# Values of heads 0 and 1 by seven half-size products, with the scores between them

## The chip, the cores and the metric

The kernel runs on one core of one Trainium2 chip. The metric is the device time of one execution in microseconds (us). Engines are named as the profile names them: PE is TensorE (matmul), PEld its weight load, DVE is VectorE, ACT is ScalarE, POOL is GpSimd, SP is the engine that issues the loads. L975 is line 975 of the kernel before.

## The reference, cut to what matters

One layer of a hybrid block over 528 tokens (16 meta tokens and 512 of the sequence), model width 1024:

```python
xn = rms_norm(h, norm_mix_g[l])
z = xn @ w_in[l]
u_rnn, u_gate, q, k, v, g_ret, ga, gb = jnp.split(z, IN_SPLITS, axis=-1)
xr = causal_dwconv(u_rnn, ...)
hr = rg_lru(xr, ...)
o_a = hr * jax.nn.gelu(u_gate)
q = rotary(q ...); k = rotary(k ...) * RET_DK ** -0.5      # 4 heads of 256
o = retention(q, k, v)                                     # v: 4 heads of 512
o_b = head_rms(o) * jax.nn.silu(g_ret)
mixed = sigmoid(ga) * (o_a @ w_branch_rnn) + sigmoid(gb) * (o_b @ w_branch_ret)
h = h + mixed @ w_out
xn = rms_norm(h, norm_ffn_g)
gate, val = jnp.split(causal_dwconv(xn @ w_up, ...), 2, axis=-1)
h = h + (gelu(gate) * val) @ w_down
out = rms_norm(h, norm_final_g)[:, N_META:]
```

Retention of a head is, in the kernel's form, `(q k^T * decay) v` over all tokens at once. The change concerns `v = xn @ w_in[:, v columns]` of the first two heads, a product of 528 tokens by 1024 by 512 for each.

## The kernel before, in words

**Precision.** Every float32 operand is written as a high and a low float16 part by `split` (L93 to L96): ACT makes the high part, and DVE the low part from the source and the high part. Each product is three matmuls (high·high, high·low, low·high). A weight goes this way from `raw` (three float32 buffers, filled by SP's loads) to `wt` (pool `wsp`, ten buffers, each with up to 1024 columns of both parts).

**Two forms of a product.** A plain one, and one with seven products of half size (the Winograd form of Strassen's scheme) in place of eight. The second needs sums of the operand blocks: for weights `fast_steps` makes them in five steps (a split of 512 columns, a split of 1024, three additions in `raw` at L262 to L264, two more splits of 1024, marked late) into four `wt` buffers; a plain unit takes two splits of 1024 into two buffers. For the tokens `make_forms(g)` makes them for half of the rows (g = 0, 1): four sums of high and low parts (L883), four sums of these (L885 to L888), and four splits, all over 544 columns, into the tiles `xs`. They are used by `fast_values` and by all gate projections.

**Stages of the mixer, in program order.** The convolution branch; the gelu branch (ten projections for `u_gate`, n = 0 to 9, with recurrence gates, decays and scans between them); `rotary`, which projects q and k of heads 0 to 3 and turns them, with `between(i)` after each, which finishes the last scans and calls `branch_a(n)` (the product hr·gelu at L775 and its split into `oa`); then

```python
    scores(0)
    values(0)
    make_forms(0)
    scores(1)
    scores(2)
    make_forms(1)
    values(1)
    scores(3)
    psum_layout(acc=2, bank=4)
    ahead[0] = 9
    for _ in retention_out(0):
        pass
    gated(0)
    for h in range(2, 4):
        ahead[0] = 12
        fast_values(h)
        ahead[0] = 9
        gated(h - 1)
```

`scores(h)` has three groups of 12 matmuls; DVE multiplies each group by the decay (L852) and ACT and DVE split it. `values(h)` runs four blocks of 24 matmuls with 512 columns (L975) and a tail of 16 for the last 16 tokens (L967). `fast_values(h)` runs seven products of 24 matmuls with 256 columns (L999) and a tail of 40 (L1033). Its product names are those of the operands: `B11`, `B21`, `B22` are blocks of the weights, `T1` to `T4` sums of them; `A11`, `A12`, `A22` are blocks of the tokens, `F3`, `F5`, `F6`, `F7` sums. The order is B11, B21, T2, T3, T1, tail, B22, T4. `retention_out(h)` multiplies the scores by the values (L1065); `gated(h)` applies the head's norm and gate.

**What sets the order.** Up to the end of the gelu branch the code fixes the order of PE, ACT and DVE (`manual_schedule`). Behind it a planner orders each engine by program order and by its own estimate of when operands are ready, and grants buffers as they come free; it pulls ready work, such as weight splits, ahead of its place. On the chip each engine then follows its order strictly. SP's loads are chained in order.

**Weights ahead.** Units (a load and its steps) are numbered in order of use: q and k of heads 0 to 3, then the value units of heads 0 and 1 (two each), then gates and values of later heads. `tick()` emits the next step, as long as the tiles of the units from the current one to that of the step are not more than `ahead[0]`; `get(u)` emits all that is left up to unit u.

**PSUM.** It has eight banks. During the rotary and scores stages they are four accumulators `acc` of two banks; `psum_layout(acc=2, bank=4)` closes these and opens two of two banks and four single ones. A new tile waits until the old ones at its place are released. `rotary` takes two accumulators for each of q and k; DVE reads each of them twice (L798, L799).

## Time and profile before

| what | value |
|---|---|
| median of 3 runs | 1056.48 us (1056.47 to 1056.61) |
| profiled execution | 1056.48 us, span 1054.8 us |
| busy: PE, weight loads, DVE, ACT, POOL | 99%, 82%, 83%, 56%, 1% of the span |
| granted clock of TensorE | 0.999 |
| first score matmul of head 0 (L845) | at 223.30 us |
| first matmul of the retention output (L1065) | at 283.05 us |

The span runs from the first to the last instruction; the time of an execution has some 1.7 us around it. Matmuls are pipelined, so a matmul's listed duration is longer than the distance from its start to the next one's; the distance is what it costs. The same holds, less strongly, for DVE and ACT. In the rows of a timeline stand start, time, engine, line, operation, what is written and read, a count, and in brackets the idle time of the engine before it with what ended it.

### The profile page before, as it was taken

What the parts mean: (1) busy time and instruction counts of PE and PEld (TensorE: products, weight loads), DVE (VectorE), ACT (ScalarE), POOL (GpSimd) and SP (SyncE); (2) the same over time, 40 slices, a digit from 0 to 9 for tenths busy, and PEclk for the clock granted to TensorE, in tenths of its full rate; (3) what the DMA queues carried; (4) which work ended last, traced back from release to release, by engine and by line L of the source; (5) the groups of instructions that cost most, each with busy time, mean ns of one, the idle gap of its engine ahead of it and who ended that gap; (6) DMA issues with size and microseconds to landing.
All of it is one profiled execution on the core that took longest, in us unless ns stands there. A gap on an engine that the chain in (4) does not pass through costs nothing.

```text
span 1054.8 us, 21439 instructions
## 1 busy us (share of the span) xinstructions
PE 1039.1 (99%) x9187; PEld 866.4 (82%) x9187; DVE 870.8 (83%) x1319; ACT 587.2 (56%) x940; POOL 6.9 (1%) x20
## 2 busy tenths in 40 slices
PE   9999999999999999999999999999999999999997
PEld 6888888865688888888888885588888888888884
DVE  6985799889579999998797785479989888988965
ACT  8668834334366757766454453375555555454432
POOL 2000000000000000000000000000000000000000
PEclk9999999999999999999999999999999999999999
DMA  9341353321013133334333355032432324114212
GB/s 296 97 131 56 121 180 121 122 83 41 2 41 120 42 106 93 97 105 152 106 106 121 120 202 179 6 115 86 156 111 90 120 81 147 54 62 146 95 41 80
DMA packets 109311, 111.52 MB, mean 106 GB/s; under 512 B 5674, under 2 KB 101136, under 8 KB 109216
## 3 DMA queue, kind: packets, MB, share of 16 engines
q1 hardware_dynamic: 108640, 109.74, 32.6%
q8 instruction: 72, 1.18, 0.5%
q10 hardware_dynamic: 288, 0.27, 0.1%
q0 software_dynamic: 288, 0.14, 0.1%
q14 instruction: 23, 0.19, 0.1%
HBM read 108.04 MB, written 2.10 MB: 104 GB/s over the span
## 4 chain that ended last, share of the span: by engine, by line
PE 84%; DVE 11%; ACT 3%; issue 1%; DMA 0%; ACTq 0%; DVEq 0%
PE ps L434 36%; PE P L1628 10%; PE pa L911 9%; PE pe L911 4%; PE ps L1345 4%; PE pm L434 3%; DVE wt L95 3%; PE ps L448 3%; PE pb L911 2%; PE ps L975 2%; PE pa L1515 2%; PE ps L1065 2%; PE pa L999 1%; ACT wt L94 1%; DVE raw L262 1%
## 5 line engine op out<-in xcount | busy, mean ns | idle before, releaser
L434 PEld LDWEIGHTS <-wt 128*128 128x128 f16 x3840 | 372.8, 97 | 51.4
L95 DVE SCALAR_TENSOR_TENSOR wt<-raw,wt 128x1024 f16<-128x1024 f32 (+2 forms) x286 | 310.9, 1102 | 59.7 <-ACT wt L94 58.5
L94 ACT ACTIVATE wt<-raw 128x1024 f16<-128x1024 f32 (+2 forms) x286 | 268.1, 959 | 127.7 <-PE P L1628 23.1
L911 PEld LDWEIGHTS <-wt 128*128 128x128 f16 x2016 | 195.3, 97 | 32.4 <-issue 5.7
L434 PE MATMUL ps<-x2h,wt 128*128 128x258 f16 (+1 forms) x1184 | 196.2, 272 | 0.0
L434 PE MATMUL ps<-xh,wt 128*128 128x258 f16 (+4 forms) x1056 | 177.0, 274 | 0.0
L434 PE MATMUL ps<-x2l,wt 128*128 128x256 f16 (+1 forms) x592 | 160.9, 272 | 0.0
L434 PE MATMUL ps<-xl,wt 128*128 128x256 f16 (+4 forms) x528 | 140.7, 274 | 0.0
L1628 PE MATMUL P<-wt,act 128*128 128x256 f16 x792 | 88.3, 273 | 0.0
L1628 PEld LDWEIGHTS <-act 128*128 128x128 f16 x792 | 77.5, 98 | 9.0
L911 PE MATMUL pa<-xs,wt 128*128 128x258 f16 x576 | 71.3, 273 | 2.0 <-ACT kept L917 1.6
L1493 DVE SCALAR_TENSOR_TENSOR cv<-ps,vt,cv 128x512 f32<-128x512 f32 x80 | 59.5, 747 | 9.1 <-ACT cv L1491 8.5
L434 PE MATMUL pm<-oa,wt 128*128 128x256 f16 (+1 forms) x480 | 54.1, 273 | 0.0
L262 DVE TENSOR_TENSOR raw<-raw 128x1024 f32<-128x1024 f32 x43 | 52.5, 1221 | 0.7
L911 PE MATMUL pa<-ob,wt 128*128 128x257 f16 x384 | 45.7, 274 | 0.6 <-ACT last L917 0.5
L1345 PE MATMUL ps<-wt,mx 128*128 128x512 f16 x192 | 44.3, 379 | 0.0
L975 PE MATMUL ps<-wt,xh 128*128 128x512 f16 x128 | 38.3, 379 | 0.7 <-ACT qk L94 0.5
L1491 ACT ACTIVATE cv<-ps,vt,vt 128x512 f32<-128x512 f32 x40 | 30.6, 767 | 11.9 <-PE ps L434 11.9
L1515 PEld LDWEIGHTS <-wt 128*128 128x128 f16 x336 | 32.6, 97 | 4.4
L1345 PEld LDWEIGHTS <-mx 128*128 128x128 f16 x192 | 17.7, 98 | 18.4
L448 PEld LDWEIGHTS <-wt 128*128 128x128 f16 x288 | 27.9, 97 | 5.0 <-issue 0.6
L1065 PE MATMUL ps<-sc,v 128*128 128x257 f16 (+4 forms) x384 | 31.7, 236 | 0.0
(328 smaller groups left out, 1475.2 us busy)
## 6 DMA issues: line engine op xcount, KB each, us to landing
raw<-in_w_in SPq DMA_DIRECT2D x36, 1024.0 KB, 5.0
raw<-in_w_up SPq DMA_DIRECT2D x24, 1024.0 KB, 5.2
raw<-in_w_down SPq DMA_DIRECT2D x48, 256.0 KB, 3.7
raw<-in_w_branch_ret SPq DMA_DIRECT2D x16, 512.0 KB, 4.9
raw<-in_w_in SPq DMA_DIRECT2D x12, 512.0 KB, 4.7
raw<-in_w_branch_rnn SPq DMA_DIRECT2D x8, 640.0 KB, 4.7
raw<-in_w_out SPq DMA_DIRECT2D x4, 1024.0 KB, 5.0
xin<-in_x SPq DMA_DIRECT2D x4, 512.0 KB, 5.7
```

Of the source, the lines that this page charges most:

```text
L94: a = nc.scalar.activation(hi, src, AF.Copy, scale=s)
L95: b = nc.vector.scalar_tensor_tensor(lo, src, s, hi, op0=ALU.mult, op1=ALU.subtract)
L262: nc.vector.tensor_tensor(pair, pair, rv[:, :, right].rearrange("p (h k) c -> p h k c", h=2), op=ALU.add)
L434: nc.tensor.matmul(half_of(ps, halves, hf), w(aw, k, col, P), src(ax, k, c0, n), start=k == 0 and (aw, ax) == (0, 0), stop=k == nk - 1 and ...
L448: mm = nc.tensor.matmul(half_of(ps, halves, hf), w(aw, k, col, P), src(ax, k, c0, n), start=k == 0 and (aw, ax) == (0, 0), stop=k == KD - ...
L911: nc.tensor.matmul(ps[:, :n], ws[k // 4](wf, aw, k % 4), src(xf_, ax, k), start=first and k == 0 and (aw, ax) == (0, 0), stop=k == last_k ...
L975: nc.tensor.matmul(pb, xf(ax, k, XF + j0, nb), w(aw, k % 4, 0, 512), start=i == 0, stop=i == 23)
L1065: nc.tensor.matmul(ps[:, hf, s0 - lo_i:257], vd, st[SCP[b][0]][:, sa, o:o + hi_i - s0], start=i == 0, stop=i == len(todo) - 1)
L1345: nc.tensor.matmul(ps[:, n], mx[k][:, a, c0:c0 + P], wo[k // 2](aw, k % 2, n * 512, 512), start=k == 0 and (a, aw) == (0, 0), stop=k == ks ...
L1493: nc.vector.scalar_tensor_tensor(vv_, taps[j], vt2[:, 48 * j + ch:48 * j + ch + 1], vv_, op0=ALU.mult, op1=ALU.add)
L1515: nc.tensor.matmul(ps[:, :258], w(wf, aw, k), x2_form(xf_, ax, k), start=first and k == 0 and (aw, ax) == (0, 0), stop=k == 3 and aw == 1, ...
L1628: nc.tensor.matmul(pd[:, 256 * tt:256 * tt + 256], t[:, ax, c0 + tt * P:c0 + tt * P + P], w(wf, aw, i), start=q % 6 == 0 and tt == 0 and i ...
```

## The change

The values of heads 0 and 1 use `fast_values` too, so `values` and the plain value units are gone. The twelve score groups are no longer stages of their own: `scores` yields after each group, and `fast_values(h)` takes the next group of `scores(2h)` and `scores(2h + 1)` after each product. The PSUM layout changes ahead of them; for h < 2 the tail's result has a single bank. `make_forms` is cut into `sum_forms` (the sums) and `split_forms` (the splits), called in the gelu branch behind the projections n = 0 and 1 (g = 0) and n = 5 and 6 (g = 1). `between` ticks once more from i = 2 on, sets `ahead[0]` to 10 at i = 3, and calls `branch_a` for n = 0 to 5 alone; n = 6 to 9 follow the four parts of `retention_out(0)`.

```diff
     def add_v(h):
-        if h >= 2:
-            u_v[h] = [unit(4, 512, [(2 * j, 0, kmaj(w_in, 4 * j + 2 * a, 2, o_v + 512 * h, 512)) for j in range(2)],
-                           fast=True) for a in range(2)]
-            return
-        u_v[h] = [unit(4, 512, [(0, 0, kmaj(w_in, 4 * a, 4, o_v + 512 * h, 512))]) for a in range(2)]
+        u_v[h] = [unit(4, 512, [(2 * j, 0, kmaj(w_in, 4 * j + 2 * a, 2, o_v + 512 * h, 512)) for j in range(2)],
+                       fast=True) for a in range(2)]
...
+    def sum_forms(g):
...
+        for i in range(2):
+            for j in range(2):
+                v = t[i, j] = work.tile([P, 2 * TW], F32, name="xt", tag="w").rearrange("p (k c) -> p k c", k=2)
+                k0, c0 = 4 * j + 2 * g, XF + TH * i
+                nc.vector.tensor_tensor(v, xh[:, k0:k0 + 2, c0:c0 + TW], xl[:, k0:k0 + 2, c0:c0 + TW], op=ALU.add)
+        a11, a12, a21, a22 = t[0, 0], t[0, 1], t[1, 0], t[1, 1]
+        nc.vector.tensor_tensor(a22, a22, a21, op=ALU.subtract)
+        nc.vector.tensor_tensor(a21, a11, a21, op=ALU.subtract)
+        nc.vector.scalar_tensor_tensor(a11, a22, -1.0, a11, op0=ALU.mult, op1=ALU.subtract)
+        nc.vector.scalar_tensor_tensor(a12, a11, -1.0, a12, op0=ALU.mult, op1=ALU.subtract)
+        x_sum_t[g] = (a12, a22, a11, a21)
+
+    def split_forms(g):
+        ks = slice(2 * g, 2 * g + 2)
+        for i, v in enumerate(x_sum_t.pop(g)):
+            xs = x_form_t[i // 2]
+            split(xs[:, 2 * (i % 2), ks], xs[:, 2 * (i % 2) + 1, ks], v, 1.0)
...
             rnn_gates(i)
+        if n in (0, 1, 5, 6):
+            (sum_forms, split_forms)[n % 5](n // 5)
...
     def between(i):
+        if i >= 2:
+            tick()
+        if i == 3:
+            ahead[0] = 10
         if i < 2:
             rnn_scan(8 + i)
-        for n in ((i,), (5, 6), (7, 8), (9,))[max(0, i - 4)]:
+        for n in (i,) if i < 6 else ():
             branch_a(n)
...
-        group([(0, 0, 0, 257), (1, 0, 257, 257)])
-        group([(0, 1, 0, T - I0[1]), (1, 2, 0, T - I0[2])])
-        group([(0, 3, 0, T - I0[3]), (1, 4, 0, T - I0[4])])
+        yield group([(0, 0, 0, 257), (1, 0, 257, 257)])
+        yield group([(0, 1, 0, T - I0[1]), (1, 2, 0, T - I0[2])])
+        yield group([(0, 3, 0, T - I0[3]), (1, 4, 0, T - I0[4])])
...
-    def fast_values(h):
+    def fast_values(h, others=()):
...
-        pa, pe, pb, pt = bank("pa"), bank("pe"), bank("pb"), acc("pv")[:, 0]
+        others = iter(others)
+        pa, pe, pb = bank("pa"), bank("pe"), bank("pb")
+        pt = bank("pv") if h < 2 else acc("pv")[:, 0]
...
             tick()
+            next(others, None)
...
-                    if h < 2 or b == 4:
+                    if b == 4:
                         vd = vt[b][:, va, d * P:(d + 1) * P]
...
-    scores(0)
-    values(0)
-    make_forms(0)
-    scores(1)
-    scores(2)
-    make_forms(1)
-    values(1)
-    scores(3)
     psum_layout(acc=2, bank=4)
+    ahead[0] = 12
+    for h in range(2):
+        fast_values(h, chain(scores(2 * h), scores(2 * h + 1)))
     ahead[0] = 9
-    for _ in retention_out(0):
-        pass
+    for n, _ in enumerate(retention_out(0)):
+        branch_a(6 + n)
     gated(0)
```

## The prediction, made before the changed kernel was run

> **What bounds the kernel now.** I read the page first (busy times, slices, chain), then the stages by windows, then the timeline of TensorE (PE) and VectorE (DVE) around the changed lines.

> ```profile
> span 1054.8 us, 21439 instructions
> PE 1039.1 (99%) x9187; PEld 866.4 (82%) x9187; DVE 870.8 (83%) x1319; ACT 587.2 (56%) x940; POOL 6.9 (1%) x20
> PE 84%; DVE 11%; ACT 3%; issue 1%; DMA 0%; ACTq 0%; DVEq 0%
> ```

> PE streams nearly all the time, so only fewer streamed columns or shorter waits can help; DVE is second and carries 11% of the chain. The profiled execution took 1056.48 us: its span of 1054.8 and 1.7 around it; that is also the median of the runs.

> ```profile
> 80.70:125.00 44.30, 44.30 (x404) 39.01 (x402) 28.55 (x36) 38.65 (x58) 0.00 (x0) 1.00 0.23 72
> 125.00:159.10 34.10, 34.10 (x309) 29.81 (x308) 34.06 (x41) 15.84 (x20) 0.00 (x0) 1.00 0.52 171
> 191.00:223.30 32.30, 32.30 (x290) 27.97 (x289) 25.32 (x36) 12.36 (x18) 0.00 (x0) 1.00 0.38 124
> 223.30:283.00 59.70, 58.77 (x368) 30.79 (x366) 50.06 (x101) 23.80 (x46) 0.00 (x0) 1.00 0.07 26
> 283.00:318.00 35.00, 34.79 (x372) 30.88 (x370) 24.22 (x45) 23.03 (x43) 0.00 (x0) 1.00 0.10 32
> ```

> Each row has a stretch, its length, the busy time of PE, of PE's weight loads, DVE, ACT and POOL, the clock, and DMA. They are: most of the gelu branch; its end and the first head's q and k (DVE full, 34.06 of 34.10); the last q and k; scores and values of heads 0 and 1 (the stage that is rebuilt); the first retention output with the first gate; all at full clock. PE has hardly any idle time to recover; DVE has some, not between 125 and 159.

> **Part 1: PE work in the rebuilt stage.**

> ```profile
> 223.30 0.93 PE L845 MATMUL ps<-qk,qk 128*128 128x257 f16 x7
> ...
> 243.12 1.05 PE L967 MATMUL ps<-wt,xlast 128*32 128x512 f16 x16
> 244.10 0.83 PE L845 MATMUL ps<-qk,qk 128*128 128x257 f16 x6
> ...
> 274.64 0.59 PE L975 MATMUL ps<-wt,xh 128*128 128x512 f16 x2
> ...
> 279.82 3.24 PE L845 MATMUL ps<-qk,qk 128*128 128x257 f16 x27
> ...
> 283.05 1.20 PE L1065 MATMUL ps<-sc,v 128*128 128x257 f16 x13
> ```

> From 223.30 to 283.05 the stage takes 59.75 us. From 274.64 to 279.82 runs one block of 24 matmuls of 512 columns: 5.18 us, 216 ns each. Eight such blocks are 41.4. The two tails (243.12 to 244.10) are 2.0. The last 33 of a head's 36 score matmuls take 279.82 to 283.05, 3.23, so 3.5 a head and 14.0 for four. Sum 57.4; the other 2.35 us are gaps. What the new form costs is seen where heads 2 and 3 already use it:

> ```profile
> 317.92 0.38 PE L999 MATMUL pa<-wt,xh 128*128 128x256 f16 x2
> ...
> 320.85 0.27 PE L999 MATMUL pa<-wt,xh 128*128 128x256 f16 x1 [0.48 <-DVE wt L95]
> ...
> 326.73 0.27 PE L999 MATMUL pa<-wt,xs 128*128 128x256 f16 x1 [0.38 <-ACT wt L94]
> ...
> 333.34 0.71 PE L1033 MATMUL pv<-wt,xlast 128*16 128x256 f16 x17
> ...
> 334.20 2.79 PE L999 MATMUL pa<-wt,xs 128*128 128x256 f16 x24
> 336.83 0.38 PE L999 MATMUL pe<-wt,xh 128*128 128x256 f16 x2
> ...
> 339.45 0.27 PE L911 MATMUL pa<-xh,wt 128*128 128x258 f16 x1
> ```

> A product of 24 takes 334.20 to 336.83, 2.63 us (109 ns a matmul). Fourteen are 36.75. The last 25 of 40 tail matmuls take 0.86 (333.34 to 334.20), so two tails 2.75. With the same scores: 53.5. The saving is 59.75 − 53.5 = 6.25 us with no gap left, 57.4 − 53.5 = 3.9 with the old gaps. I take 6.25 and charge the waits one by one. Head 2's call took 21.53 us (317.92 to 339.45) against 7·2.63 + 1.38 = 19.8: 1.8 us of waits for weights.

> [...]

> **Part 2: the tokens' sums move into the gelu branch.** There the orders of PE, ACT and DVE are fixed by the code.

> ```profile
> 235.96 1.99 DVE L883 TENSOR_TENSOR xt<-xh,xl 128x544 f32<-128x544 f16 x3
> ...
> 88.71 0.71 DVE L665 TENSOR_TENSOR rnn<-rnn,gi 128x528 f32<-128x528 f32 x1 [1.06 <-ACT gi L663]
> 89.65 1.23 DVE L95 SCALAR_TENSOR_TENSOR wt<-raw,wt 128x1024 f16<-128x1024 f32 x1 [0.24 <-ACT wt L94]
> 94.91 0.71 DVE L665 TENSOR_TENSOR rnn<-rnn,gi 128x528 f32<-128x528 f32 x1 [4.03 <-ACT gi L663]
> ...
> 123.95 1.23 DVE L95 SCALAR_TENSOR_TENSOR wt<-raw,wt 128x1024 f16<-128x1024 f32 x1 [4.30 <-ACT wt L94]
> ...
> 155.59 1.29 DVE L775 TENSOR_TENSOR rnn<-rnn 128x514 f32<-128x514 f32 x2
> 156.80 0.68 DVE L799 TENSOR_TENSOR t<-ps,rope 128x514 f32<-128x514 f32 x1
> 157.41 0.68 DVE L798 TENSOR_TENSOR t<-ps,rope 128x514 f32<-128x514 f32 x1
> ...
> 158.61 0.69 DVE L799 TENSOR_TENSOR t<-ps,rope 128x514 f32<-128x514 f32 x1
> ```

> Three sums span 1.99 with ends overlapping by about 0.08, so one costs 0.635. Sixteen sums and eight remainders are 24·0.635 = 15.2 us of DVE, and eight ACT copies. The stage's DVE idle is 44.30 − 28.55 = 15.75, of which about 3.0 lies before the first sum can start (behind the row at 88.71). The 4.03 and 4.30 gaps are filled; of what remains I reckon 3.6 usable, since most of it is waits for ACT, which the copies make later. So 11.9 fit and DVE enters the scans 3.3 us late. It then has no idle until past 159. On ACT the second group's copies wait for DVE's last sum, with a weight copy, five roots and a gate's eviction queued behind, about 2.2 us late; ACT has 18 us idle in the next row (15.84 of 34.10) and PE four accumulators there, so nothing is paid.

> What is late next is the reading of q0. Its second accumulator is last read by L798 at 157.41 (ends 158.1), its first by L799 at 158.61.

> ```profile
> 159.15 0.27 PE L434 MATMUL ps<-xl,wt 128*128 128x256 f16 x1
> ```

> PE begins q1 at 159.1 and needs the second accumulator: 1.0 us of slack. Late by 3.3, PE waits 2.3 us once (the next unit is shifted with it). Bounds: 0, if the planner puts the multiplications of L775, which nothing needs yet, behind these reads; 3.3, if the slack goes too. I take 2.3, since the planner had put them ahead though DVE was late.

> **Part 3: weights.** Each of the four value units changes from 2 splits of 1024 to one of 512, three of 1024 and three sums.

> ```profile
> 201.86 1.23 DVE L95 SCALAR_TENSOR_TENSOR wt<-raw,wt 128x1024 f16<-128x1024 f32 x1 [2.83 <-ACT wt L94]
> ...
> 212.47 1.23 DVE L95 SCALAR_TENSOR_TENSOR wt<-raw,wt 128x1024 f16<-128x1024 f32 x1 [2.12 <-ACT wt L94]
> ...
> 223.58 1.22 DVE L262 TENSOR_TENSOR raw<-raw 128x1024 f32<-128x1024 f32 x1
> 224.72 0.70 DVE L799 TENSOR_TENSOR t<-ps,rope 128x528 f32<-128x528 f32 x1
> ...
> 226.57 0.70 DVE L799 TENSOR_TENSOR t<-ps,rope 128x528 f32<-128x528 f32 x1
> ...
> 231.10 1.23 DVE L852 SCALAR_TENSOR_TENSOR sf<-ps,dec 128x257 f32<-128x257 f32 x3
> ...
> 235.36 0.68 DVE L95 SCALAR_TENSOR_TENSOR v<-ps,v 128x512 f16<-128x512 f32 x1
> ```

> 1024 columns cost 1.14 (223.58 to 224.72), 512 about 0.6 (155.59 to 156.80 is two): 6.4 us of DVE a unit against 2.3, +16.4 for four, and three more additions a head, +3.6. The 2.83 and 2.12 us waits show the splits paced by weight tiles that PE frees. Ten tiles exist, so head 0's eight can be ready at the end of k3: 12.8 us instead of the 9.1 that all four units cost there now, against 7 us idle in the 191 row. Cost 0; the q and k reads cover it, and without that cover the first product waits, at most the 3.7 more. The six extra ticks only bring these steps forward.

> Head 1 is the tight place: head 0 holds eight tiles until its tail, so two of head 1's tiles can be made before, six after. From the end of k3 to head 1's second half of T2, PE has 26.8 + 8.9 = 35.7 us (a head is 7·2.63 + 1.38 + two heads' scores 7.0; then three products but a half, 6.6, and two score groups of 1.17). DVE owes: the rest of k3 4.3 (seven of 0.617; three lie between 224.72 and 226.57), scores of two heads 7.8 (231.10 to 235.36 less one sum of 0.64 is 3.6 a head, 3.9 with two small copies), head 0's three adds and five splits 4.8, head 1's units 12.8, two of head 2's score groups 3.3, one add and split 1.2, one oa split 0.6: 34.8. It fits by 0.9. I charge 1.8 once, what head 2's call paid under a full DVE. Bounds 0 (score groups fill the hole) and 5.7: at the 84% that DVE reaches in this stage now (50.06 of 59.70), 34.8 takes 41.4.

> **Part 4, small.** The PSUM layout now changes while k3 is being read; the last read ends 4.0 us after 223.30 (226.57 + 0.70). First product and first score group, 3.8, cover it: 0, and up to 4.0 if the planner gives them those banks. The four oa steps moved into the retention output are 4.8 us of DVE, beside 10.8 idle in the 283 row; the gate's weights, now later there, are some 6 more. That cover just holds; if not, up to 3 us. On SP, which issues in order, no step is passed by another:

> ```profile
> raw<-in_w_in SPq DMA_DIRECT2D x36, 1024.0 KB, 5.0
> raw<-in_w_in SPq DMA_DIRECT2D x12, 512.0 KB, 4.7
> ```

> four loads of the first kind become eight of the second, issued a unit ahead: 0. The sums issue none.

> **Sum.** 1056.48 − 6.25 + 2.3 + 1.8 = 1054.3 us. What a measurement tells from no change is 0.2%, 2.1 us; the forecast sits on that line.

> **Rivals.**
> A, cover everywhere: the reads of q0 are placed ahead and scores fill head 1's hole: 1056.48 − 6.25 + 0 to 2 gives 1050.2 to 1052.6. For it: PE waits are short wherever it was planned. Against: DVE at 34.06 of 34.10. Chance 0.17.
> B, the gain is eaten: waits of 5 to 8 us, since DVE gets about 20 us more work where it had idle time in small pieces: 1055.4 to 1058.6. Chance 0.16.
> C, slower, by one mechanism: head 1's weights come late because their tiles are held by head 0. At 84% DVE use PE waits 5.7 before T2 and, the backlog not being caught up, another 1.8 in that call; with 2.3 before, 1056.48 − 6.25 + 9.8 = 1060.0. It decides once all waits pass 8.4 us. For it: the 0.9 us margin; against: head 2's call, with weights as late and no scores to fill in, lost 1.8. Chance 0.22 for 1058.6 to 1063.
> D, weight loads pace the products: 144 more at 97 ns, wholly unhidden, are 14.0: 1064. The 109 ns spacing excludes it for L999; chance 0.02. [...]

> **How the numbers follow.** Forecast 0.43, over 1052.6 to 1055.4, of which 0.25 beyond 0.2%. Faster 0.17 + 0.25 = 0.42; same 0.18 + 0.14 = 0.32; slower 0.02 + 0.22 + 0.02 = 0.26. The range 1051 to 1060.5 leaves out about 0.05 below and 0.12 above; the likeliest case alone is 1052.6 to 1055.4.

> **What would show it.** Right: L975 gone, L999 at x672 with 24 matmuls in 2.63; xt sums near 90 and 118 us; one PE wait of about 2 us for a DVE read of q0's accumulator near 159; waits on wt in head 1's call, some 2 us together; the first retention output starting at 283.05 − 6.25 + 2.3 + 1.8 = 280.9. Wrong: no wait near 159 (A), or waits on wt of over 5 us between the two heads' calls (C), or PE waiting on DVE reads throughout q and k (B).

## The result, and the profile after

The changed kernel takes 1060.30 us (median of 7 runs, 1058.74 to 1060.49) against 1056.52 before (7 runs, 1056.37 to 1056.69) on the same chip: ratio 1.0032, 95% interval 1.0022 to 1.0041. It is slower by 3.8 us; the forecast was 1054.3. The profiled execution took 1060.44, its span 1058.7.

The page of the changed kernel, first lines and the shares of the chain that ended last:

```profile
span 1058.7 us, 21861 instructions
PE 1036.5 (98%) x9379; PEld 882.1 (83%) x9379; DVE 891.2 (84%) x1345; ACT 594.5 (56%) x954; POOL 6.9 (1%) x20
PE 79%; DVE 15%; ACT 3%; issue 2%; DMA 0%; DVEq 0%; ACTq 0%
```

PE is busy for 2.6 us less than before, and the span is 3.9 us longer: the saving is there, and more than that went into waits, for DVE by the chain (15% instead of 11%). The same stretches as in the prediction, by windows:

```profile
80.70:125.00 44.30, 44.30 (x404) 39.01 (x402) 38.74 (x54) 38.90 (x58) 0.00 (x0) 1.00 0.23 72
125.00:159.10 34.10, 34.10 (x309) 29.81 (x308) 34.09 (x39) 19.49 (x26) 0.00 (x0) 1.00 0.43 140
159.10:223.30 64.20, 60.92 (x546) 52.56 (x544) 62.46 (x90) 23.11 (x32) 0.00 (x0) 1.00 0.28 88
223.30:283.00 59.70, 55.86 (x554) 46.60 (x552) 45.01 (x90) 25.75 (x47) 0.00 (x0) 0.97 0.20 68
```

Up to 159.1 PE loses nothing. Then it loses 3.3 us among q and k (64.20 less 60.92), where it lost nothing before:

```profile
159.10:223.30 64.20, 64.20 (x577) 55.85 (x576) 56.01 (x80) 25.92 (x36) 0.00 (x0) 1.00 0.39 126
```

It loses 3.8 us more in the stretch of the rebuilt stage (59.70 less 55.86), where the clock now has a mean of 0.97. What PE waited for (total, times, longest):

```profile
PE ps L432 <- DVE t L825: 3.3, 2, 1.8
PE pa L979 <- DVE t L825: 2.7, 1, 2.7
...
PE ps L876 <- DVE sf L883: 1.1, 2, 1.0
...
PE pa L979 <- DVE wt L96: 0.9, 2, 0.5
PE pa L979 <- ACT wt L95: 0.6, 2, 0.4
```

In the new line numbers L432 is the projection of q and k, L825 and L826 the reads of their accumulators by `rotary` (L799 and L798 before), L979 the products of `fast_values`, L876 a score group, L883 its read. The two rows on `wt` stand in the profile before with the same totals (0.9 and 0.6): they are those of heads 2 and 3. The values of heads 0 and 1 wait for no weight. The timeline of PE at these places:

```profile
159.15 0.28 PE L432 MATMUL ps<-xh,wt 128*128 128x264 f16 x1
160.94 0.28 PE L432 MATMUL ps<-xh,wt 128*128 128x256 f16 x1 [1.52 <-DVE t L825]
...
173.44 0.29 PE L432 MATMUL ps<-xh,wt 128*128 128x264 f16 x1 [1.75 <-DVE t L825]
...
227.02 0.28 PE L432 MATMUL ps<-xh,wt 128*128 128x264 f16 x1
230.02 0.38 PE L979 MATMUL pa<-wt,xh 128*128 128x256 f16 x2 [2.72 <-DVE t L825]
...
233.96 0.42 PE L979 MATMUL pa<-wt,xl 128*128 128x256 f16 x1
234.17 1.62 PE L876 MATMUL ps<-qk,qk 128*128 128x257 f16 x12
235.63 0.38 PE L979 MATMUL pb<-wt,xh 128*128 128x256 f16 x2
...
266.73 0.60 PE L979 MATMUL pe<-wt,xs 128*128 128x256 f16 x4
268.30 0.22 PE L876 MATMUL ps<-qk,qk 128*128 128x144 f16 x1 [0.96 <-DVE sf L883]
...
286.89 3.28 PE L1046 MATMUL ps<-sc,v 128*128 128x257 f16 x39
```

q1 starts 1.7 us late and k1 another 1.9, so k3 ends at 227.1 instead of 223.3. The first value product waits 2.9 us more, to 230.02, and then its 24 matmuls take 4.15 us (to 234.17) where 2.63 is the price at full clock. The retention output starts at 286.89 instead of 283.05: 3.84 us late, which is the whole result. In the rows, [2.72 <-DVE t L825] counts idle time from the listed end of the matmul before; counted from when the next matmul could have started, 0.11 us behind 227.02, it is 2.9. The clock in these stretches (the eighth figure, behind the busy times):

```profile
227.10:230.00 2.90, 0.20 (x2) 0.01 (x1) 2.87 (x5) 1.06 (x1) 0.00 (x0) 1.00 0.39 149
230.00:232.00 2.00, 1.98 (x14) 1.61 (x15) 2.00 (x5) 0.75 (x2) 0.00 (x0) 0.75 0.00 0
232.00:234.00 2.00, 2.00 (x12) 1.37 (x10) 2.00 (x4) 0.53 (x1) 0.00 (x0) 0.50 0.00 0
234.00:236.00 2.00, 2.00 (x18) 1.70 (x17) 1.93 (x4) 0.60 (x1) 0.00 (x0) 0.89 0.00 0
```

Behind these 2.9 us of idle time PE ran at half clock for a while: the trace's clock record has 0.50 from 231.02 to 234.43, and 1.00 on both sides. In five of the seven runs (1060.17 to 1060.49) the mean clock of the execution is 0.997 or 0.998, in the other two (1058.74 and 1058.93) 0.999. That these two were spared the low clock is inferred, mostly from their times: 0.998 also stands beside runs of the kernel before, and no timeline of these two was kept. And DVE, in the order it worked:

```profile
119.94 2.63 DVE L756 TENSOR_TENSOR xt<-xh,xl 128x544 f32<-128x544 f16 x4
122.60 0.72 DVE L758 TENSOR_TENSOR xt<-xt 128x544 f32<-128x544 f32 x1
123.36 0.73 DVE L759 TENSOR_TENSOR xt<-xt 128x544 f32<-128x544 f32 x1
...
130.33 1.42 DVE L680 TENSOR_TENSOR rnn<-rnn 128x528 f32<-128x528 f32 x2
...
167.31 3.71 DVE L802 TENSOR_TENSOR rnn<-rnn 128x514 f32<-128x514 f32 x6
170.93 1.22 DVE L96 SCALAR_TENSOR_TENSOR wt<-raw,wt 128x1024 f16<-128x1024 f32 x1
172.06 0.70 DVE L826 TENSOR_TENSOR t<-ps,rope 128x528 f32<-128x528 f32 x1
...
222.99 0.70 DVE L825 TENSOR_TENSOR t<-ps,rope 128x528 f32<-128x528 f32 x1
226.69 0.69 DVE L96 SCALAR_TENSOR_TENSOR wt<-raw,wt 128x512 f16<-128x512 f32 x1 [3.00 <-ACT wt L95]
227.42 1.22 DVE L260 TENSOR_TENSOR raw<-raw 128x1024 f32<-128x1024 f32 x1
228.56 0.70 DVE L826 TENSOR_TENSOR t<-ps,rope 128x528 f32<-128x528 f32 x1
229.18 0.70 DVE L825 TENSOR_TENSOR t<-ps,rope 128x528 f32<-128x528 f32 x1
...
230.41 0.70 DVE L826 TENSOR_TENSOR t<-ps,rope 128x528 f32<-128x528 f32 x1
```

The first scan multiplication (L680) starts at 130.33; in the timeline before it is the first of these rows, and the second is a split ahead of k3's reads there:

```profile
125.09 0.70 DVE L682 TENSOR_TENSOR rnn<-rnn 128x528 f32<-128x528 f32 x1
...
222.85 0.69 DVE L95 SCALAR_TENSOR_TENSOR wt<-raw,wt 128x512 f16<-128x512 f32 x1 [1.80 <-ACT wt L94]
```

DVE is 5.2 us late at the scans. At 167.31 six multiplications of the gelu branch (L802) stand in its order ahead of the reads of k0. At 226.69 it is not DVE that is short of time: it has stood still for 3.0 us in front of a weight split whose high part ACT could not write, and k3's last three reads stand behind that split and a sum (L260) in DVE's order. ACT's own row says for what it waited:

```profile
226.03 0.63 ACT L95 ACTIVATE wt<-raw 128x512 f16<-128x512 f32 x1 [3.68 <-PE ps L432]
```

The split had to wait for a tile that PE's k projection was still reading.

### The profile page after: what moved, and what is told of

It is laid out like the page before. It is cut to its first block, busy times and chain, and to the rows that moved or that the text cites. A ratio compares the mean times of both kernels' runs of the same rounds, so it can differ in the third digit from the quotient of the medians.

```text
span 1058.7 us, 21861 instructions
## 1 busy us (share of the span) xinstructions
PE 1036.5 (98%) x9379; PEld 882.1 (83%) x9379; DVE 891.2 (84%) x1345; ACT 594.5 (56%) x954; POOL 6.9 (1%) x20
## 4 chain that ended last, share of the span: by engine, by line
PE 79%; DVE 15%; ACT 3%; issue 2%; DMA 0%; DVEq 0%; ACTq 0%
PE ps L432 31%; PE P L1604 10%; PE pa L919 9%; DVE wt L96 5%; PE pe L919 4%; PE ps L1321 4%; PE pm L432 3%; PE ps L446 3%; PE pa L979 3%; PE pb L919 2%; PE pa L1491 2%; PE ps L1046 2%; PE pe L979 1%; ACT wt L95 1%; DVE raw L260 1%
## 5 line engine op out<-in xcount | busy, mean ns | idle before, releaser
L432 PEld LDWEIGHTS <-wt 128*128 128x128 f16 x3840 | 372.6, 97 | 55.2 <-DVE t L825 3.8
L96 DVE SCALAR_TENSOR_TENSOR wt<-raw,wt 128x1024 f16<-128x1024 f32 (+2 forms) x294 | 318.1, 1098 | 48.7 <-ACT wt L95 47.8
L95 ACT ACTIVATE wt<-raw 128x1024 f16<-128x1024 f32 (+2 forms) x294 | 274.2, 955 | 128.2 <-DVE raw L260 24.8
L919 PEld LDWEIGHTS <-wt 128*128 128x128 f16 x2016 | 195.3, 97 | 32.4 <-issue 5.7
L432 PE MATMUL ps<-x2h,wt 128*128 128x258 f16 (+1 forms) x1184 | 196.2, 272 | 0.0
L432 PE MATMUL ps<-xh,wt 128*128 128x258 f16 (+4 forms) x1056 | 177.3, 274 | 3.3 <-DVE t L825 3.3
L432 PE MATMUL ps<-x2l,wt 128*128 128x256 f16 (+1 forms) x592 | 160.9, 272 | 0.0
L432 PE MATMUL ps<-xl,wt 128*128 128x256 f16 (+4 forms) x528 | 140.6, 274 | 0.0
L260 DVE TENSOR_TENSOR raw<-raw 128x1024 f32<-128x1024 f32 x47 | 57.4, 1221 | 0.7
L432 PE MATMUL pm<-oa,wt 128*128 128x256 f16 (+1 forms) x480 | 54.1, 273 | 0.0
L979 PEld LDWEIGHTS <-xs 128*128 128x128 f16 x384 | 37.0, 98 | 8.4 <-issue 4.1
L1467 ACT ACTIVATE cv<-ps,vt,vt 128x512 f32<-128x512 f32 x40 | 30.6, 766 | 11.9 <-PE ps L432 11.9
L1491 PEld LDWEIGHTS <-wt 128*128 128x128 f16 x336 | 32.6, 97 | 4.4
L979 PE MATMUL pa<-wt,xs 128*128 128x256 f16 x288 | 34.1, 273 | 1.0 <-ACT wt L95 0.6
L262 DVE TENSOR_TENSOR raw<-raw 128x512 f32<-128x512 f32 x47 | 32.3, 687 | 0.8
## 6 DMA issues: line engine op xcount, KB each, us to landing
raw<-in_w_in SPq DMA_DIRECT2D x32, 1024.0 KB, 5.0
raw<-in_w_up SPq DMA_DIRECT2D x24, 1024.0 KB, 5.2
raw<-in_w_in SPq DMA_DIRECT2D x20, 512.0 KB, 4.8
raw<-in_w_branch_ret SPq DMA_DIRECT2D x16, 512.0 KB, 4.8
raw<-in_w_out SPq DMA_DIRECT2D x4, 1024.0 KB, 5.0
xin<-in_x SPq DMA_DIRECT2D x4, 512.0 KB, 5.8
```

The source lines that it names most:

```text
L95: a = nc.scalar.activation(hi, src, AF.Copy, scale=s)
L96: b = nc.vector.scalar_tensor_tensor(lo, src, s, hi, op0=ALU.mult, op1=ALU.subtract)
L260: nc.vector.tensor_tensor(pair, pair, rv[:, :, right].rearrange("p (h k) c -> p h k c", h=2), op=ALU.add)
L262: nc.vector.tensor_tensor(rv[:, low, left], rv[:, low, left], rv[:, low, right], op=ALU.add)
L432: nc.tensor.matmul(half_of(ps, halves, hf), w(aw, k, col, P), src(ax, k, c0, n), start=k == 0 and (aw, ax) == (0, 0), stop=k == nk - 1 and ...
L919: nc.tensor.matmul(ps[:, :n], ws[k // 4](wf, aw, k % 4), src(xf_, ax, k), start=first and k == 0 and (aw, ax) == (0, 0), stop=k == last_k ...
```

## The experiments

Two causes were proposed. Theory 1: the first value product has its PSUM bank (`pa`) in a place that k3's accumulator holds; it waits for k3's reads, and the low clock follows from the idle time. Theory 2: the sums in the gelu branch make DVE late for the reads of q0 and k0, by itself and whatever the values do. The rivals: rival C of the prediction (late weights), or a stage that would be as slow with any bank. All were timed in five rounds beside the kernel before, whose median was 1056.56 to 1056.68 in the three groups.

**e1: the two pools in the other order.**

```diff
-    psum_layout(acc=2, bank=4)
+    psum_layout(bank=4, acc=2)
```

> The changed kernel with one line swapped: the four single PSUM banks are opened ahead of the two double accumulators, so the first product's bank lies where q3's accumulators lay and not k3's. Theory 1 (a bank of k3 that DVE still reads holds up the first product, and the idle time then lowers PE's clock): the 2.9 us wait before the first product goes, the product takes 2.6 instead of 4.0 us, and the time falls by some 4 us from 1060.3 to 1056. Rival (DVE is overloaded, the wait only shows it): the same time is lost a little later, at the first score group or at the third product, and the time stays within 1 us of 1060.

Measured: 1061.94 us (1061.45 to 1062.74), ratio 1.0051, interval 1.0039 to 1.0064. Slower still. The chain of PE's waits says why:

```profile
PE pa L979 <- DVE krep L865: 4.0, 1, 4.0
```

`pa` lands in the other of k3's two accumulators, the one that is read last. The row names `krep`, a copy that reads no PSUM, because it comes directly behind that last read in DVE's order. The read, L826, ends at 230.97 and the product starts at 231.11, 0.14 us later, as it starts 0.14 us behind L825 in the changed kernel (229.88 and 230.02). As a test of theory 1 the edit missed its aim; it did show that the wait goes with the bank: 4.0 us in place of 2.7.

**e2: the kernel before, with only the tokens' sums and their splits moved into the gelu branch.**

```diff
...
+        if n in (0, 1, 5, 6):
+            (sum_forms, split_forms)[n % 5](n // 5)
...
-    make_forms(0)
...
-    make_forms(1)
```

> The kernel before with one part of the change alone: the tokens' sums and their splits in the gelu branch; values of heads 0 and 1 by the plain products and everything else as before. Theory 2 (the sums put DVE 5 us behind and PE waits for its reads of q0 and k0): the two waits at q1 and k1 appear here too, 3 to 4 us together; the stage of scores and values gains at most its 2.35 us of gaps, so the time is 1057 to 1060. Rival (the waits at q1 and k1 come from the added ticks and the later oa steps): no such waits, and the time is at or below 1056.5.

Measured: 1060.22 us (1060.10 to 1060.48), ratio 1.0034, interval 1.0021 to 1.0046. The two waits of q1 and k1 are those of the changed kernel:

```profile
PE ps L434 <- DVE t L827: 3.3, 2, 1.8
```

So this half of the change costs 3.6 us alone, slightly more than the 1057 to 1060 expected allowed. The stage of scores and values, with the sums gone from it, gives nothing back: it takes 59.8 us (227.11 to 286.91), as before. Theory 2 holds, for the size too.

**e3: the changed kernel, with the multiplication of `branch_a` behind the last rotary read issued.**

```diff
-        nc.vector.tensor_mul(g, g, half_x.pop(n)[:, T0:])
+        with tc.issue_after(last_read[0]):
+            nc.vector.tensor_mul(g, g, half_x.pop(n)[:, T0:])
...
-            nc.vector.tensor_mul(t2[:, :n], run_of(pp[1 - m], halves), sn)
+            last_read[0] = nc.vector.tensor_mul(t2[:, :n], run_of(pp[1 - m], halves), sn).ins
```

> The changed kernel, with the multiplications of the gelu branch's output (branch_a) kept behind DVE's last read of the rotary accumulators of the unit before them. Theory 2 in its sharper form (in the order of DVE these multiplications, which nothing needs yet, stand ahead of the reads): the wait at k1 (1.9 us) goes, the one at q1 (1.7) shrinks to about 0.5, and the time falls by 3 us to about 1057.3. Rival (DVE is short of time whatever the order): the waits move to the next units, and the time stays at 1060.

Measured: 1057.47 us (11 runs, 1056.05 to 1057.85), ratio 1.0004, interval 0.9995 to 1.0013; 2.8 us less than the changed kernel. No wait is left at k1 and 0.8 at q1: most of theory 2's cost came from these multiplications standing ahead of the reads once the sums had made DVE late, not from the sums' time as such. The wait of the first product remains, and the runs fall into two groups, five of 1056.05 to 1056.50 at a mean clock of 0.999 and six of 1057.47 to 1057.85 at 0.996 to 0.998. Each group is 2.5 to 2.7 us below the like group of the changed kernel, by medians; the 2.8 has a little of the groups' shares in it.

**e5: the changed kernel, with 13 matmuls on data of no use ahead of the first product,** to keep the array busy while it waits (they add work and change no output).

```diff
+    pw = acc("warm2")
+    for _ in range(13):
+        nc.tensor.matmul(pw[:, 0], xh[:, 0, XF:XF + P], xh[:, 0, XF:XF + 512], start=True, stop=True)
```

> The changed kernel with 13 matmuls of 512 columns, whose result nothing reads, ahead of the first product, in an accumulator of its own. Theory 1b (the clock of PE falls behind the idle 2.9 us): PE is busy over the wait, the granted clock stays at 1.00, the first product takes 2.6 instead of 4.0 us, and the time falls by about 1.4 us to the 1058.8 that some executions of the changed kernel show. Rival (the first product is slow for its operands): it still takes 4.0 us, and the time is 1060 or more.

Measured: 1064.69 us (1064.26 to 1065.53), ratio 1.0078, interval 1.0064 to 1.0092.

```profile
231.03 4.67 PE L1157 MATMUL warm<-xh 128*128 128x512 f16 x13 [3.87 <-DVE t L826]
235.53 0.38 PE L979 MATMUL pa<-wt,xh 128*128 128x256 f16 x2
```

They had got one of k3's accumulators themselves, waited 4.0 us for it (from 226.99, 0.11 us behind the start of k3's last matmul), and took 4.5 us where 13 at 216 ns are 2.8; the product behind them ran at full clock. So the low clock is no property of the product: here it met the 13 matmuls that came first after the idle time. As a cure it failed: the expectation had been 1058.8.

**e6: another layout.** `pa`, `pe` and the first score group get the banks of q3's accumulators; the banks of k3's go to tiles that are needed later. Behind the two value calls the pools have their old sizes again.

```diff
-        pa, pe, pb = bank("pa"), bank("pe"), bank("pb")
-        pt = bank("pv") if h < 2 else acc("pv")[:, 0]
+        pa, pe = bank("pa"), bank("pe")
+        if h < 2:
+            pb, pt = (psum["late"].tile([P, 512], F32, name=nm, tag="late") for nm in ("pb", "pv"))
+        else:
+            pb, pt = bank("pb"), acc("pv")[:, 0]
...
-    psum_layout(acc=2, bank=4)
+    psum_layout(late=2, acc=2, bank=2)
...
+    psum_layout(bank=4, acc=2)
     ahead[0] = 9
```

> The changed kernel with the PSUM pools of the two value calls opened in another order and number (two late banks, two accumulators, two banks), so that the first product's bank and the first score group lie on q3's accumulators, and only the second product and the second group on k3's. The earlier swap had put the first product on k3's other accumulator, which is read last, so it was no test. Theory 1 (the bank alone makes the first product wait): it starts at once behind k3, takes 2.5 us at full clock, and the time falls by the 2.9 us of the wait and the 1.4 us of the low clock, to about 1056. Rival (DVE is overloaded here): the wait appears at the second product or the first groups, and the time stays above 1058.5.

Measured: 1055.96 us (11 runs, 1055.91 to 1056.32), ratio 0.9994, interval 0.9985 to 1.0003; 4.3 us less than the changed kernel, and one group of runs.

```profile
226.96 0.28 PE L432 MATMUL ps<-xh,wt 128*128 128x264 f16 x1
227.08 0.38 PE L982 MATMUL pa<-wt,xh 128*128 128x256 f16 x2
...
282.26 0.27 PE L982 MATMUL pe<-wt,xl 128*128 128x256 f16 x1
282.37 0.27 PE L919 MATMUL pa<-xh,wt 128*128 128x258 f16 x1
```

The first product follows k3 with no wait. From 227.08 to 282.37, where the last one ends and a gate's matmuls begin, the stage takes 55.3 us; in the changed kernel it took 59.76 (227.13 to 286.89). The wait did not turn up again at the second product or the first score group, as it would have if DVE were too slow with any bank. Theory 1 holds.

**e7: e6 and e3 together.**

> The layout of the run before together with the gelu output's multiplications kept behind the rotary reads. If the two causes are separate, their gains add: 2.9 less again, about 1053.2, below the kernel before. Rival (both delays come from one DVE backlog, so mending one mends or moves the other): less than half of the second gain is seen, 1054.7 or more.

Measured: 1053.37 us (1053.32 to 1053.69), ratio 0.9969, interval 0.9958 to 0.9981: faster than before. The two gains add (4.3 and 2.8 off 1060.30 give 1053.2; the step from e6 to e7 is 2.6, as in e3 by like groups), so they are separate causes.

**e8: the changed kernel, with the weight steps of the first value call issued behind k3's last read.**

```diff
-        run()
+        with tc.issue_after(held[0]) if held[0] else nullcontext():
+            run()
...
+        held[0] = last_read[0] if h == 0 else None
```

> The changed kernel, its layout kept, with every weight step that is emitted in the first value call kept behind DVE's last read of k3's accumulators. Theory 1c (in DVE's order a 512-column weight split, whose tile PE frees only near the end of k3, and an addition stand ahead of these reads; DVE idles 3.0 us there): the reads follow the end of k3 directly, the second accumulator is free some 1.3 us after it, the first product's wait falls from 2.9 to about 1.4 us, the low clock shortens or goes, and the time falls by 1.5 to 3 us, to 1057.5 to 1059. Rival (the weight split is needed that early): the weights of the second head come later and the time is 1060 or more.

Measured: 1057.54 us (11 runs, 1057.43 to 1057.71), ratio 1.0008, interval 0.9999 to 1.0017; 2.8 us less than the changed kernel.

```profile
228.65 0.38 PE L983 MATMUL pa<-wt,xh 128*128 128x256 f16 x2 [1.51 <-DVE t L829]
...
226.90:228.60 1.70, 0.24 (x3) 0.00 (x0) 1.42 (x3) 1.06 (x1) 0.00 (x0) 1.00 0.00 0
228.60:230.60 2.00, 1.95 (x18) 1.79 (x19) 2.00 (x3) 0.65 (x1) 0.00 (x0) 1.00 0.00 0
```

With the reads first, 1.5 us of idle time is left of 2.7, and the clock stays at 1.00. The weight steps that stood in front of the reads made 1.2 us of that wait, and so the low clock.

**e9: e7, with the second group's sums and splits made in `between(4)` and `between(5)` instead of the gelu branch.**

```diff
-        if n in (0, 1, 5, 6):
+        if n in (0, 1):
...
+        if i in (4, 5):
+            (sum_forms, split_forms)[i % 2](1)
```

> The layout and the kept-back multiplications, and the second group's sums and splits moved from the gelu branch to between the last rotary units (i = 4 and 5), where DVE has idle time. Theory 2 (half of the backlog at the scans, about 2.6 us, goes): no wait at q1, and 1.0 us less than without the move, about 1052. Rival (DVE's idle time there is waits for tiles and cannot be used): reads of later units come late, and the time is the same or more than without the move.

Measured: 1053.97 us (1053.87 to 1054.18), ratio 0.9974, interval 0.9964 to 0.9984. The wait at q1 is gone, yet it is 0.6 us slower than e7, where about 1 us less was expected: the work came back as a later wait. The second product (`pb`, on a bank of k3's) now stands behind k3's reads:

```profile
229.00 0.39 PE L987 MATMUL pb<-wt,xh 128*128 128x256 f16 x2 [1.53 <-DVE t L829]
```

**e10: e9 and e8 together.**

> The other layout, the multiplications behind the rotary reads, the second group's sums behind head 2's q, and the weight steps of the first value call behind k3's last read. If the 0.6 us that the kernel without the last edit lost to the one with the sums in the gelu branch is the wait of the second product for k3's reads, which stood behind weight splits, holding these steps back takes that wait (1.5 us) away: 1052.3 to 1052.8, no wait at q1, stage start 227. Rival: DVE is simply full up to the end of k3, and what is held back is late for the products: 1053.4 or more, with waits on wt or on sums of weights in head 0's call.

Measured: 1052.58 us (1052.42 to 1052.94), ratio 0.9962, interval 0.9949 to 0.9976, the fastest of all. The first product starts at 223.41, as the scores did before (the expectation's 227 was wrong), with no wait on k3's reads anywhere; of waits in the stage two are left, both of a score group, one of 1.3 us:

```profile
PE ps L883 <- DVE sf L890: 1.4, 2, 1.3
```

**e11: e7 and e8 together,** the sums staying in the gelu branch.

> The other layout, the multiplications behind the rotary reads and the weight steps of the first value call behind k3's last read; the sums stay in the gelu branch. With this layout the first product doesn't wait for k3, so holding the weight steps back has nothing to win: 1053.4 (same as without it). Rival: the weight steps come later and the products of head 0 wait for them, 1054 to 1055; or the reads of k3 still delay the first score group, then 1052.6.

Measured: 1053.58 us (1053.50 to 1053.74), ratio 0.9971, interval 0.9960 to 0.9983; 0.2 us above e7. With e6's layout, and the sums where the change puts them, holding the steps back has nothing to win. It pays only where the reads are late (e8, e10).

## Why the prediction was wrong, point by point

The terms of the sum, against the changed kernel's trace; 53.3 us for the stage's work is 14 products of 2.62 (268.36 to 270.98 in the timeline), two tails of 1.2, and score groups of 1.32, 1.71 and 0.53 four times.

| term | predicted | measured |
|---|---|---|
| work of the rebuilt stage, from 59.75 | −6.25 (53.5) | −6.4 (53.3) |
| waits inside it for weights | +1.8 | +1.9 (the rest of the stage's 59.76), but not for weights |
| DVE's backlog, at the end of k3 | +2.3 | +3.8 (223.3 to 227.1) |
| k3's accumulator under the first product | 0 | +2.9 |
| low clock after that wait | not in it | +1.7 (4.15 less 2.62, and 0.14 in the score group) |
| sum | −2.2 | +3.9 |

**Part 1 was right.** At full clock 24 matmuls of 256 columns take 2.62 us, in heads 0 and 1 as in heads 2 and 3: 109 ns a matmul, against 216 for one of 512 columns in the blocks of the kernel before.

**Part 4 failed, on the PSUM layout,** and this decided the sign. The step charged 0, because "First product and first score group, 3.8, cover it", with the bound "up to 4.0 if the planner gives them those banks". They were given: with `acc=2, bank=4` the bank of `pa` lies on an accumulator of k3, whose last read (L825 at 229.18) ends just before `pa` starts. k3's reads are no later than before (the last, L826 at 230.41, ends 4.0 us after k3, as in the prediction's reckoning); what is new is who stands on them. Before the change the score group took an accumulator that q3 had left. e6 takes the cause away, and 4.3 us with it; e1 moves it to the later accumulator, and the wait becomes 4.0. With this step right the change would not have lost: e6, without the wait and the low clock, comes out level with the kernel before (0.7 us below it, within the interval). The order of the pools decides the banks, as e1 and e6 show, but it does not say alone which of them k3 holds: e1's expectation took it from the order and was wrong.

**The clock was in no term.** Behind the wait of 2.9 us the low clock cost 1.7 more in the profiled execution, and by their times in four more of the seven runs.

**Part 2 was right in kind and too small.** The sums stand where they were expected (89.55 and 119.94), and q1 waits for a read of q0 near 159. Two sizes were off. DVE is 5.2 us late at the scans, not 3.3: four of the eight sums of a group depend on one another and cost 0.76 each (122.60 to 123.36), not 0.635, and by 125 DVE had taken on 10.2 us (28.55 to 38.74), not 11.9. And "once, the next unit is shifted with it" was wrong: the multiplications that the planner had put ahead of q0's reads came ahead of k0's, six in a row, and k1 waited 1.9 as well. The lower bound, 0 "if the planner puts the multiplications behind these reads", is nearly what e3 shows when that is done by hand: 0.8 at q1 and none at k1.

**Part 3: the size was right, the reason not.** 1.8 us was charged for head 1's weights. In e6 the stage exceeds its work by 2.0 us, of which 1.1 is score groups that wait for their accumulator (the longer wait lies between 266.73 and 268.30 in the changed kernel), since DVE's read of the scores there, at 267.82, stands behind two weight splits; no product of these heads waits for `wt`. The other 0.9 was not traced to a wait. The prediction also did not ask what the weight steps do to DVE's order: a split, for which DVE stands still, and a sum lie ahead of k3's reads. They are steps of the first value call that the planner pulled forward, not those of the six extra ticks, since e8 holds back that call's steps alone and both then lie behind the reads. Before the change a split and a sum lay there too (222.85 and 223.58), and nothing waited for those reads; with the new layout it was paid (e8).

**The rivals.** The time fell on rival C's 1060.0, but not by its mechanism: DVE is busy for 45.0 of 59.7 us in this stage, less than before, and head 1's weights are in time. The price that rival asked, waits of over 8.4 us, was reached by other waits: 3.8, 2.9, 1.7 and 1.9. Rival A, cover everywhere, is nearest to e10: with the orders and the banks put right the change gives 1052.6, within A's 1050.2 to 1052.6.

What stays open: why some runs seem to have been spared the low clock, and whether the score group's last 1.3 us in e10 can be had.

## What to carry to other kernels

When a PSUM layout changes between stages, write down which tile of the new layout lies on which of the old, and who reads the old one last: the first tiles that PE writes belong on the banks that are read out first. Work that is moved "under cover" on a strictly ordered engine is to be priced by what then stands behind it in that order, above all behind an instruction that itself waits; the moved sums made DVE 5 us late and cost 3.6, of which 2.5 to 2.8 came back by reordering instructions that nobody needed yet. A change that brings a saving and a new wait is best judged apart: here e7 and e10 keep the saving.

## What the runs showed of the hardware that was not expected

The low clock lasted 3.41 us in the changed kernel (231.02 to 234.43). In the other three it lasted 3.4 us by an estimate from the mean clocks of their windows, which together lack 1.7 us of full clock in each (e3: 0.91 over 2.9 us, then 0.50 and 0.78 over 2.0 each; e1: 0.51 and 0.64 over 2.0 each; e5: 0.69, 0.50 and 0.96 over 2.0 each). It cost PE 1.7 us in the changed kernel, and 1.4 in e3 (3.99 us for the product instead of 2.62), where 0.6 us of it fell into the gap. Why some runs with this gap seem to have been spared was not shown: no trace of such a run was kept.
